# Squares over three weight blocks, a unit in three visits, two accumulators moved, a bias put behind

## The chip, the cores and the metric

The kernel runs on one core of a Trainium2 chip. The metric is the device time of one execution in microseconds: 1636.31 us, the median of three runs (1636.26 to 1636.46). The engines are named as the profile names them: PE (TensorE) with its weight loads PEld, DVE (VectorE), ACT (ScalarE), POOL (GpSimd) and SP (SyncE, which issues the loads).

## The reference

One decoder layer on 288 tokens (256 of a prompt, 8 x 4 of samples), all in float32, width 2048. Cut to what the change touches:

```python
mod = (silu(c) @ w_ada + b_ada).reshape(n, 6, 1, 2048)   # sh_m, sc_m, gt_m, sh_f, sc_f, gt_f
h = rms(x, g_mix) * (1 + sc_m) + sh_m                     # rms: x * rsqrt(mean(x*x) + eps) * gain
proj = h @ w_in                                           # 2048 x 9216, split into seven parts
```

After it come a convolution mixer, a spatial gating mixer, their merge, an output projection and a feed-forward network; the change leaves all of those as they are.

## The kernel before

Activations lie transposed: 128 features on the partitions, 288 tokens along the row, 16 feature tiles (`k`) for the width of 2048. A matmul takes 128x128 weights and a row of 288 tokens (298 where ten columns more are carried along). Full float32 precision is made from two halves: every weight `w` and every activation `a` is split into a rounded `hi` and a remainder `lo`, and a *triple* of matmuls adds `wh*ah`, `wh*al` and `wl*ah` into one accumulator in PSUM (`triple`, L248). For the weights, ACT makes `hi` (a cast) and DVE makes `lo` (a subtraction), four 128x128 parts at a time (`feed`, L267). A finished accumulator is copied out by ACT or DVE (`sinkA`; `ON_VECTOR` lists the tiles that DVE takes). Seven buffers of 1 MB (`raw`) hold loaded weights.

The head of the program, some 70 us, has its order written out by hand for PE, ACT, DVE and SP:

- The condition `c` goes through silu into `cs` (L151 to L153), and *units* of the modulation (`ada`, L407) multiply it with their weights. The first, `a0`, is the first real work of PE, after 24 fill matmuls (`warm`); it and the second, `a1`, give the first two feature tiles their scale and shift (`scaled_tile`). The third unit, `aC` (eight blocks), gives features 2 to 4 theirs; a run of its blocks between weight blocks is a *visit*.
- The square sum that the normalisation needs is not there yet when PE starts. So the first 48 output tiles of `w_in` are multiplied for features 0 and 1 with input that is scaled but not normalised (*rootless*), and the normalisation is applied to the sums later. The weight blocks in order: `w0` (feature 0, 16 output tiles), `wK` (feature 1 for the last six of those), then `wA` in blocks of eight output tiles with two triples each: four rootless blocks (output tiles 16 to 47), then three whose input is normalised (`h1`).
- `squares1` says after which tile of which block ACT squares a group of feature tiles of `x`, and DVE adds the squares up. Its two buffers are two of the seven weight buffers. `root` then queues the sums over features (`sums1`, matmuls with ones, L202), the diagonal matrix of the roots (`diagonal`) and its broadcast over the partitions (`norm1`, L235), each after a number of triples; `norm1` starts the normalised input of features 0 and 1.
- `SquareSum` and what follows the head are not changed.

PSUM has four accumulators called main, three called misc and one for the units. In `w0`, tiles 0 to 3 use all four main ones, and tiles 4 and 5 wait for two of them to be read out.

A load is issued seven steps ahead of its use, in the order of the steps, and SP issues in that order only: a load that waits for its buffer holds all behind it. A weight block's parts are split when no more than `lead` triples of given parts are left (12 unless it says otherwise); the cast then stands in ACT's queue ahead of the evictions that come after it.

Of the kernel before, what the change touches and what calls it, by code (L numbers as in the profile page):

```python
# [11 lines left out]
ALU = mybir.AluOpType  # L12
# [9 lines left out]
NC = 9  # L22
# [28 lines left out]
SINGLE = 10  # L51
FIRST = 16
ROOTLESS = 48
LATER = 48
ON_VECTOR = (2, 5, 7, 9, 10, 12, 14, 16, 18, 20, 21, 22, 24, 28)
XCUT = (0, 1, 2, 6, 10, 14, 16)

STREAMS = {
# [37 lines left out]
def _body(tc, nc, d, pc, pw, pslot, ptmp, pps):  # L96
# [15 lines left out]
    def psmain():  # L112
        return pps.tile([P, 512], F32, tag="main", name=nm("pm"), bufs=4)

    def psmisc():
        return pps.tile([P, 512], F32, tag="misc", name=nm("px"), bufs=3)

    V, A, G, PE, SY = nc.vector, nc.scalar, nc.gpsimd, nc.tensor, nc.sync
# [7 lines left out]
    bada = cp1[:, C_BADA : C_BADA + 96]  # L126
# [23 lines left out]
    ctt = const("ctt", [P, 16, NC])  # L150
    A.activation(ctt, ct, AF.Tanh, scale=0.5)  # L151
    V.scalar_tensor_tensor(ctt, ctt, 1.0, ct, ALU.add, ALU.mult)
    V.tensor_scalar(cs[:, :, :NC], ctt, 0.5, None, ALU.mult)  # L153
    mod = const("mod", [P, 96, NC])
    gm1 = const("gm1", [P, 16, NC])
    gm2 = const("gm2", [P, 16, NC])
# [1 line left out]
    end = const("end", [P, 2, TU - TP])  # L158
    G.memset(end, 0.0)
    bada1 = const("bada1", [P, 2])  # L160
    V.tensor_scalar(bada1, bada[:, 16:18], 1.0, None, ALU.add)


    class SquareSum:
# [3 lines left out]
        def add(self, a, cuts=((0, T),)):  # L168
            q = tmp() if self.last is not None else ptmp.tile([P, T], F32, tag="acc", name=nm("acc"), bufs=1)
            for o, e in cuts:  # L170
                A.activation(q[:, o:e], a[:, o:e], AF.Square)  # L171
            if self.last is not None:
                if self.acc is None:
                    self.acc = self.last
                else:
                    V.tensor_tensor(self.acc, self.acc, self.last, ALU.add)  # L176
            self.last = q
# [115 lines left out]
    def later(f, gap=0):  # L293
        if not pending:
            since[0] = 0
        pending.append((f, gap))
# [6 lines left out]
    def behind(a, b):  # L303
        tc.add_manual_dep(
            a.ins,
            b.ins.name,
            mybir.DependencyInfo(mybir.DependencyClass.NoSync, mybir.DependencyReason.DATA),
            reason="program order",
        )
# [228 lines left out]
    class OneTile(Blk):  # L538
        held = {}

        def run(self):
            a, turn, hooks = self.rhs(self.k0), [], self.hooks
            (ah, al) = a
            for j in range(self.nm):
                if (self.name, j) == ("w0", 0):
                    pss = [psmain() for _ in range(4)]
                    for i, ps in enumerate(pss):
                        PE.matmul(ps[:, :TU], self.parts[i][0], ah, start=True, stop=False)
                    for i, ps in enumerate(pss):
                        PE.matmul(ps[:, :TU], self.parts[i][1], ah, start=False, stop=False)  # L550
                if self.name == "wK":
                    ps = OneTile.held.pop(j)
                    triple(ps[:, :TU], self.parts[j], a, False, True, True)
                elif j < 4:
                    ps = pss[j]
                    PE.matmul(ps[:, :TU], self.parts[j][0], al, start=False, stop=True)
                    counted()
                else:
                    ps = psmisc() if SINGLE <= j < FIRST - 4 else psmain()
                    triple(ps[:, :TU], self.parts[j], a, True, j < SINGLE, True)  # L560
                if self.name == "wK" or j < SINGLE:
                    self.sink(j, ps)
                    evicted(self, j)
                else:
                    OneTile.held[j - SINGLE] = ps
                drain()
                for f in hooks.get(j, ()):
                    f()
# [51 lines left out]
    def squares1():  # L620
        qa, qb = (pw.tile([P, 2048], F32, tag="raw", name=nm("q"), bufs=RAW) for _ in range(2))
        for q in (qa, qb):
            G.memset(q[:, 7 * T : 7 * T + 1], 0.0)

        def part_of(q, o, n):
            return q[:, o * T : (o + n) * T].rearrange("p (k t) -> p k t", t=T)

        q1, q0, q2, q4 = part_of(qa, 0, 4), part_of(qa, 4, 2), part_of(qb, 0, 4), part_of(qb, 4, 2)

        def square(q, a, b):  # L630
            return lambda: A.activation(q, x[:, a:b, :], AF.Square)

        def add(o, q):
            return lambda: V.tensor_tensor(o, o, q, ALU.add)

        S["sq"] = q1[:, 0]
        return {
            ("wK", 0, 4): square(q0, 0, 2),
            ("wA", 0, 0): square(q1, 2, 6),
            ("wA", 0, 1): add(q1[:, 0:2], q0),  # L640
            ("wA", 0, 2): square(q2, 6, 10),
            ("wA", 0, 3): add(q1, q2),
            ("wA", 0, 5): square(q2, 10, 14),
            ("wA", 0, 6): square(q4, 14, 16),
            ("wA", 0, 7): add(q1, q2),
            ("wA", 1, 0): add(q1[:, 0:2], q1[:, 2:4]),
            ("wA", 1, 2): add(q1[:, 0:2], q4),
            ("wA", 1, 4): add(q1[:, 0], q1[:, 1]),
        }

    def sums1():
# [13 lines left out]
    def pre_h1(k0, k1):  # L665
        def scaled(k):
            def f():
                made[k] = normed(k, S["rb1"])

            return f  # L670

        return Do(lambda: jobs.extend(scaled(k) for k in range(k0, k1)), None)
# [59 lines left out]

    def first_tile():
        low = []
        ev = a0[1].copied()
        w0.split(1, low)
        warm(2)
        scaled_tile(0, ev, lambda: low[0]())
        w0.split(1)
        S["given"], S["used"] = 8, 0  # L740
        S["feed"] = [w0, wK] + wA + wB + wX + wS + wC
# [15 lines left out]
    def mk_h1(k0, k1):  # L757
        def f():
            gm_of(k0, k1)
            if S.get("paced") is not None:  # L760
                return make_h1(k0, k1)
            modulate(range(k0, k1), lambda k: normed(k, S["rb1"]), gm1, 0, h1)

        return Do(f)
# [3 lines left out]
    def sinkA(m, ps):  # L768
        t = slot(shape=(P, TU) if m < ROOTLESS else (P, T))
        part[m] = t[:, :T]  # L770
        w = T
        if m < ROOTLESS:
            raws[m], w = t, TU
        if m not in ON_VECTOR if m < 32 else m % 2 or m % 8 == 4:
            A.copy(t[:, :w], ps[:, :w])  # L775
        else:
            V.tensor_copy(t[:, :w], ps[:, :w])
# [269 lines left out]
    for b in wA[:many]:  # L1047
        b.width = TU
    w0.cut = 512
    w0.lead, wK.lead, wA[0].lead, wA[1].lead = 6, 3, 4, 6  # L1050
    wA[0].cut = wA[1].cut = wA[2].cut = 1024

    steps = [Do(lambda: warm(24)), a0[0], Do(lambda: warm(8)), a0[1]]
    steps += [Do(first_tile), Do(lambda: warm(6))]

    def root():
        later(sums1, 1)
        later(lambda: diagonal(S["r1"]), 6)
        later(norm1, 4)

    plan = {4: [Do(root, None)], 5: aC[:4], 6: [pre_h1(2, 5)], 7: aC[4:] + [mk_h1(2, 5)]}
    steps += at([w0, wK] + wA, plan)
    steps += at(wB, {2: aD[:4], 3: [pre_h1(5, 8)], 4: aD[4:] + [mk_h1(5, 8)]})
    free = Do(lambda: None, None)
# [214 lines left out]
```

## Time and profile before

| | |
|---|---|
| median of three runs | 1636.31 us |
| the profiled execution's own time | 1637.67 us |
| its span, first to last instruction | 1635.9 us |
| PE busy | 1621.4 us (99%) |
| PE weight loads busy | 1547.1 us (95%) |
| DVE busy | 1016.8 us (62%) |
| ACT busy | 739.7 us (45%) |
| granted TensorE clock, mean | 0.998 |

Times in the views are microseconds from the span's start. In a timeline a row gives start, length, engine, line, operation, what is written and read (buffer numbers left out), the count of merged instructions, and in brackets the idle time of the engine ahead of it with the one that ended it. A row of grouped instructions gives busy time and mean nanoseconds of one, then the idle time ahead. A row of waits gives the total, the count and the longest. Matmuls overlap: one lasts 0.30 us in the records, while the next starts 0.13 to 0.14 us after it. A row of DMA issues gives size and time from issue to landing.

### The profile page before, as it was taken

The numbers are of one execution on the slowest core, as the hardware profiler recorded it, in microseconds if no ns is written. First come the engines' busy times: TensorE is split into PE (matmuls) and PEld (weight loads), VectorE is DVE, ScalarE is ACT, GpSimd is POOL, SyncE is SP. The second block draws the span as 40 slices with busy tenths as digits, with TensorE's granted clock in tenths as the row PEclk, the third lists the DMA queues.
The fourth block names the chain that finished last, engine by engine and source line by source line (L and its number), as shares of the span: only waits on it lengthen the run. The fifth ranks groups of instructions, "written<-read, shape, count | busy, mean of one in ns | idle before, by whom it ended". The sixth has DMA issues, their size and how long they took to land.

```text
span 1635.9 us, 31039 instructions
## 1 busy us (share of the span) xinstructions
PE 1621.4 (99%) x12353; PEld 1547.1 (95%) x12353; DVE 1016.8 (62%) x2191; ACT 739.7 (45%) x1364; POOL 20.8 (1%) x66
## 2 busy tenths in 40 slices
PE   9999999999999999999999999999999999999997
PEld 7899899988998999999998999999999999999997
DVE  5677688877755567667844555555555555555565
ACT  5543344643444434456743444444444444444453
POOL 0000000000000000011000000000000000000000
PEclk9999999999999999999999999999999999999999
DMA  8877775767786767744576556543464434644341
GB/s 342 316 309 277 293 265 204 265 255 281 291 316 258 277 243 287 270 165 158 209 304 252 199 169 208 177 155 124 160 219 168 163 125 160 224 156 172 111 156 58
DMA packets 59425, 357.57 MB, mean 219 GB/s; under 512 B 6640, under 2 KB 9872, under 8 KB 28560
## 3 DMA queue, kind: packets, MB, share of 16 engines
q1 hardware_dynamic: 58992, 355.45, 59.1%
q8 instruction: 96, 1.57, 0.4%
q14 instruction: 49, 0.40, 0.1%
q10 hardware_dynamic: 288, 0.15, 0.0%
HBM read 352.48 MB, written 3.09 MB: 217 GB/s over the span
## 4 chain that ended last, share of the span: by engine, by line
PE 96%; DMA 1%; DVE 1%; ACT 1%; issue 0%; DVEq 0%; ACTq 0%
PE pm L250 30%; PE pm L253 30%; PE pm L255 30%; PE ada L418 5%; DMA raw<-in_wA 1%; DMA cp<-in_cpack 0%; DVE x L1020 0%; PE pm L618 0%; ACT hi L500 0%; PE px L250 0%; PE px L253 0%; PE px L858 0%; DVE lo L506 0%; PE px L202 0%; PE px L899 0%
## 5 line engine op out<-in xcount | busy, mean ns | idle before, releaser
L250 PE MATMUL pm<-s,hi 128*128 128x288 f32 (+1 forms) x3752 | 1110.1, 296 | 1.3 <-ACT s L775 1.3
L253 PE MATMUL pm<-s,hi 128*128 128x288 f32 (+1 forms) x3752 | 1106.4, 295 | 0.2 <-DVE s L345 0.2
L255 PE MATMUL pm<-s,lo 128*128 128x288 f32 (+1 forms) x3738 | 1102.3, 295 | 0.6 <-DVE lo L269 0.5
L500 ACT CAST hi<-raw 128x512 fp32r<-128x512 f32 (+1 forms) x963 | 588.5, 612 | 815.8 <-PE pm L253 791.6
L506 DVE TENSOR_TENSOR lo<-raw,hi 128x512 fp32r<-128x512 f32 (+1 forms) x849 | 578.4, 681 | 448.2 <-ACT hi L500 430.8
L250 PEld LDWEIGHTS pm<-s,hi 128*128 128x128 f32 x3752 | 706.0, 188 | 21.2 <-issue 15.7
L253 PEld LDWEIGHTS pm<-s,hi 128*128 128x128 f32 x3752 | 705.5, 188 | 0.5 <-DVE s L345 0.4
L255 PEld LDWEIGHTS pm<-s,lo 128*128 128x128 f32 x3738 | 703.4, 188 | 1.3 <-DVE lo L269 1.3
L269 DVE TENSOR_TENSOR lo<-raw,hi 128x512 fp32r<-128x512 f32 (+1 forms) x113 | 75.8, 673 | 33.1 <-ACT hi L500 32.2
L418 PE MATMUL ada<-raw,cs 128*32 128x512 f32 (+2 forms) x832 | 88.4, 563 | 0.5 <-DVE cs L153 0.5
L418 PEld LDWEIGHTS ada<-raw,cs 128*32 128x32 f32 x832 | 24.1, 109 | 46.7 <-issue 43.6
L806 DVE TENSOR_TENSOR s<-pm,s 128x288 f32<-128x288 f32 x72 | 32.8, 456 | 14.5 <-PE pm L255 14.4
L362 DVE SCALAR_TENSOR_TENSOR x<-pm,mod,x 128x256 f32<-128x256 f32 x80 | 38.0, 475 | 2.7 <-PE pm L255 2.7
L319 ACT CAST s<-t 128x288 fp32r<-128x288 f32 (+1 forms) x76 | 32.6, 433 | 12.5 <-DVE t L838 5.8
L321 DVE TENSOR_TENSOR s<-t,s 128x288 fp32r<-128x288 f32 (+1 forms) x76 | 34.6, 458 | 5.9 <-ACT s L319 5.9
L985 DVE SCALAR_TENSOR_TENSOR t<-t,pm 128x288 f32<-128x288 f32 x42 | 19.1, 454 | 16.0 <-PE pm L255 16.0
L798 DVE TENSOR_TENSOR s<-pm,s 128x288 f32<-128x288 f32 x48 | 21.8, 454 | 10.7 <-PE pm L255 9.5
L368 DVE TENSOR_TENSOR t<-pm,mod 128x32 f32<-128x32 f32 x80 | 15.3, 191 | 18.1 <-PE pm L255 18.0
L783 DVE SCALAR_TENSOR_TENSOR s<-pm,s 128x256 f32<-128x256 f32 x48 | 23.0, 480 | 4.1 <-PE pm L255 4.1
L171 ACT ACTIVATE t<-x 128x288 f32<-128x288 f32 (+2 forms) x31 | 13.5, 437 | 20.5 <-DVE x L371 17.3
L789 DVE TENSOR_TENSOR s<-s,rb 128x288 f32<-128x288 f32 x48 | 21.5, 447 | 0.0
L176 DVE TENSOR_TENSOR acc<-acc,t 128x288 f32<-128x288 f32 x34 | 15.4, 454 | 8.2 <-ACT t L171 8.2
(150 smaller groups left out, 482.1 us busy)
## 6 DMA issues: line engine op xcount, KB each, us to landing
raw<-in_fi SPq DMA_DIRECT2D x84, 1024.0 KB, 4.9
raw<-in_a SPq DMA_DIRECT2D x64, 1024.0 KB, 9.2
raw<-in_f SPq DMA_DIRECT2D x64, 704.0 KB, 4.1
raw<-in_wD SPq DMA_DIRECT2D x36, 1024.0 KB, 4.9
raw<-in_aE SPq DMA_DIRECT2D x16, 1024.0 KB, 10.0
raw<-in_wo SPq DMA_DIRECT2D x16, 1024.0 KB, 5.0
raw<-in_wC SPq DMA_DIRECT2D x19, 768.0 KB, 4.4
raw<-in_pa SPq DMA_DIRECT2D x8, 1024.0 KB, 5.0
```

Source lines behind the costliest of these rows:

```text
L250: PE.matmul(out, wh, ah, start=first, stop=False)
L253: end_ = PE.matmul(out, wh, al, start=False, stop=turn and last)
L255: end_ = PE.matmul(out, wl, ah, start=False, stop=last)
L269: lows.pop(0)[1]()
L319: A.copy(hi, a)
L321: V.tensor_tensor(lo, a, hi.bitcast(F32), ALU.subtract)
L362: V.scalar_tensor_tensor(x[:, m, :TP], ps[:, :TP], mod[:, gt0 + m, 0:1], x[:, m, :TP], ALU.mult, ALU.add)
L418: PE.matmul(acc[32 * j : 32 * j + 32, :w], cs[:, kt, :], self.raw[:, o : o + w], start=(kt < ks), stop=(kt >= 16 - ks), tile_position=(0, ...
L500: A.copy(hi, self.raw[:, s * 128 : e * 128])
L506: sub()
L783: V.scalar_tensor_tensor(t[:, :TP], ps[:, :TP], t[:, T : T + 1], t[:, :TP], ALU.add, ALU.add)
L806: V.tensor_tensor(a, ps[:, :T], a, ALU.add)
```

## The change

Four edits, all in the head. The operation that adds one to the bias of the first scales (`bada1`) is issued later, and told to stand behind the one that writes `cs`. Tiles 4 and 5 of `w0` take misc accumulators. The squares and their additions are put at other tiles, the last two additions in the third `wA` block, with the sums ten triples into that block; the leads of the first two `wA` blocks and the list of the tiles that DVE copies out change with them (20 of the 48 rootless tiles were DVE's, now 21). The eight blocks of the third unit come in visits of two, three and three, after the third, fourth and fifth `wA` block, in place of four and four after the third and fifth.

```diff
@@ -52,7 +52,7 @@
-ON_VECTOR = (2, 5, 7, 9, 10, 12, 14, 16, 18, 20, 21, 22, 24, 28)
+ON_VECTOR = (2, 5, 7, 9, 10, 12, 14, 18, 19, 22, 23, 26, 27, 30, 32, 35, 37, 41, 43, 45, 47)
@@ -150,7 +150,7 @@
-    V.tensor_scalar(cs[:, :, :NC], ctt, 0.5, None, ALU.mult)
+    cs_made = V.tensor_scalar(cs[:, :, :NC], ctt, 0.5, None, ALU.mult)
...
-    V.tensor_scalar(bada1, bada[:, 16:18], 1.0, None, ALU.add)
@@ -556,7 +555,7 @@
-                    ps = psmisc() if SINGLE <= j < FIRST - 4 else psmain()
+                    ps = psmisc() if SINGLE <= j < FIRST - 4 or j < 6 else psmain()
@@ -636,16 +635,16 @@
             ("wK", 0, 4): square(q0, 0, 2),
-            ("wA", 0, 0): square(q1, 2, 6),
-            ("wA", 0, 1): add(q1[:, 0:2], q0),
-            ("wA", 0, 2): square(q2, 6, 10),
-            ("wA", 0, 3): add(q1, q2),
-            ("wA", 0, 5): square(q2, 10, 14),
-            ("wA", 0, 6): square(q4, 14, 16),
+            ("wA", 0, 1): square(q1, 2, 6),
+            ("wA", 0, 3): add(q1[:, 0:2], q0),
+            ("wA", 0, 5): square(q2, 6, 10),
             ("wA", 0, 7): add(q1, q2),
-            ("wA", 1, 0): add(q1[:, 0:2], q1[:, 2:4]),
-            ("wA", 1, 2): add(q1[:, 0:2], q4),
-            ("wA", 1, 4): add(q1[:, 0], q1[:, 1]),
+            ("wA", 1, 1): square(q2, 10, 14),
+            ("wA", 1, 3): add(q1, q2),
+            ("wA", 1, 4): square(q4, 14, 16),
+            ("wA", 1, 6): add(q1[:, 0:2], q1[:, 2:4]),
+            ("wA", 2, 0): add(q1[:, 0:2], q4),
+            ("wA", 2, 3): add(q1[:, 0], q1[:, 1]),
@@ -732,6 +731,7 @@
     def first_tile():
         low = []
+        behind(V.tensor_scalar(bada1, bada[:, 16:18], 1.0, None, ALU.add), cs_made)
@@ -771,7 +771,7 @@
-        if m not in ON_VECTOR if m < 32 else m % 2 or m % 8 == 4:
+        if m not in ON_VECTOR if m < ROOTLESS else m % 2 or m % 8 == 4:
@@ -1047,18 +1047,18 @@
-    w0.lead, wK.lead, wA[0].lead, wA[1].lead = 6, 3, 4, 6
+    w0.lead, wK.lead, wA[0].lead, wA[1].lead = 6, 3, 6, 8
...
     def root():
-        later(sums1, 1)
+        later(sums1, 10)
...
-    plan = {4: [Do(root, None)], 5: aC[:4], 6: [pre_h1(2, 5)], 7: aC[4:] + [mk_h1(2, 5)]}
+    plan = {4: [Do(root, None)], 5: aC[:2], 6: aC[2:5] + [pre_h1(2, 5)], 7: aC[5:] + [mk_h1(2, 5)]}
```

**SP's queue from the third unit's first block on.** `in_aC` is the third unit, `in_wA` the weight blocks, the first of them here the fourth rootless one. Before:

```order
L400 DMA raw_164<-in_aC 128x1536
L400 DMA raw_183<-in_aC 128x1536
L400 DMA raw_230<-in_aC 128x1536
L400 DMA raw_363<-in_aC 128x1536
L484 DMA raw_404<-in_wA 128x2048
L484 DMA raw_502<-in_wA 128x2048
L400 DMA raw_602<-in_aC 128x1536
```

Now:

```order
L399 DMA raw_163<-in_aC 128x1536
L399 DMA raw_182<-in_aC 128x1536
L483 DMA raw_230<-in_wA 128x2048
L399 DMA raw_366<-in_aC 128x1536
L399 DMA raw_405<-in_aC 128x1536
L399 DMA raw_502<-in_aC 128x1536
L483 DMA raw_600<-in_wA 128x2048
```

The fourth rootless block's load moves ahead of two of the unit's blocks, and the next weight block's load moves behind one more of them. The buffers move with it: the fourth rootless block takes that of the first (`raw_121`), and the one after it takes that of the first squares (`q_123`).

**DVE's queue around the sums.** `q` are the squares, `lo` the remainders of weights, `s<-pm` the copies out of accumulators, `e<-px` the first operation on the finished sums. Before (`raw_131` and `raw_136` are the second and third rootless block):

```order
L634 TENSOR_TENSOR q_124<-q_124,q_125 128x1152
L777 COPY s_514<-pm_504 128x298
L634 TENSOR_TENSOR q_124<-q_124 128x576
L269 TENSOR_TENSOR lo_513<-raw_131,hi_511 128x512
L634 TENSOR_TENSOR q_124<-q_124,q_125 128x576
L269 TENSOR_TENSOR lo_536<-raw_131,hi_534 128x512
L269 TENSOR_TENSOR lo_539<-raw_136,hi_537 128x512
L269 TENSOR_TENSOR lo_554<-raw_136,hi_552 128x512
L777 COPY s_565<-pm_557 128x298
L634 TENSOR_TENSOR q_124<-q_124 128x288
L269 TENSOR_TENSOR lo_577<-raw_136,hi_575 128x512
L215 TENSOR_SCALAR e_613<-px_608 128x3
```

Now (`raw_135` is the third rootless block, `raw_230` the fourth):

```order
L633 TENSOR_TENSOR q_123<-q_123,q_124 128x1152
L268 TENSOR_TENSOR lo_550<-raw_135,hi_548 128x512
L268 TENSOR_TENSOR lo_574<-raw_135,hi_572 128x512
L777 COPY s_585<-pm_577 128x298
L633 TENSOR_TENSOR q_123<-q_123 128x576
L268 TENSOR_TENSOR lo_597<-raw_135,hi_595 128x512
L777 COPY s_610<-pm_602 128x298
L633 TENSOR_TENSOR q_123<-q_123,q_124 128x576
L268 TENSOR_TENSOR lo_622<-raw_230,hi_620 128x512
L777 COPY s_645<-pm_635 128x298
L633 TENSOR_TENSOR q_123<-q_123 128x288
L268 TENSOR_TENSOR lo_644<-raw_230,hi_642 128x512
```

The last three additions stood among the remainders of the second block and the first of the third; now they stand behind all remainders of the third block, and the last one behind the first remainder of the fourth. Lines of the changed kernel between L161 and L734 are lower by one.

## The prediction

> **What bounds the kernel now.** The page came first: who ends last.
>
> ```profile
> PE 96%; DMA 1%; DVE 1%; ACT 1%; issue 0%; DVEq 0%; ACTq 0%
> ```
>
> The chain of waits is TensorE's own work, so a change of order can only gain what TensorE waits, and it moves no instruction after about 68 us. The view of TensorE's waits from 75 us to the end has as its longest:
>
> ```profile
> PE pm L253 <- DVE s L345: 0.2, 1, 0.2
> ```
>
> Everything to be had is therefore earlier. The timeline of weight loads shows each of those waits, with the idle time in brackets:
>
> ```profile
> 15.93 0.19 PEld L250 LDWEIGHTS pm<-s,hi 128*128 128x128 f32 x1 [0.33 <-ACT s L775]
> 16.76 0.19 PEld L250 LDWEIGHTS pm<-s,hi 128*128 128x128 f32 x1 [0.39 <-ACT s L775]
> 25.03 0.19 PEld L252 LDWEIGHTS px<-s,lo 128*128 128x128 f32 x1 [0.52 <-DVE lo L269]
> 31.19 0.19 PEld L255 LDWEIGHTS pm<-s,lo 128*128 128x128 f32 x1 [0.21 <-DVE lo L269]
> 33.66 0.19 PEld L255 LDWEIGHTS pm<-s,lo 128*128 128x128 f32 x1 [0.78 <-DVE lo L269]
> 38.90 0.19 PEld L255 LDWEIGHTS pm<-s,lo 128*128 128x128 f32 x1 [0.28 <-DVE lo L269]
> 47.73 0.19 PEld L250 LDWEIGHTS pm<-s,hi 128*128 128x128 f32 x1 [1.05 <-ACT s L775]
> 49.01 0.30 PEld L235 LDWEIGHTS px<-t,ones 128*128 128x128 f32 x2 [0.84 <-DVE t L229]
> 65.58 0.19 PEld L250 LDWEIGHTS pm<-s,hi 128*128 128x128 f32 x1 [0.53 <-ACT s L775]
> ...
> 64.98 0.29 PE L255 MATMUL pm<-s,lo 128*128 128x288 f32 x1
> 65.58 0.40 PE L250 MATMUL pm<-s,hi 128*128 128x288 f32 x1 [0.30 <-ACT s L775]
> ```
>
> The last two rows scale the brackets. The matmuls start 0.60 apart where 0.13 is the step, so the wait costs 0.46; the weight load's bracket says 0.53. I take 0.08 off each bracket. The matmul after a wait takes 0.40 instead of 0.30, so a restart costs another 0.10. The wait at 25.03 stands behind the second scaled tile, whose rows do not move; I leave it as it is.
>
> **The change, part by part.**
>
> *Bias put behind.* At the start:
>
> ```profile
> 1.23 5.88 PE L618 MATMUL pm<-wb 128*128 128x288 bf16 x24 [1.23 <-POOL wb L612]
> 5.47 0.32 ACT L151 ACTIVATE ctt<-ct 128x144 f32<-128x144 f32 x1 [2.54 <-DMA ct<-in_c]
> 6.91 0.17 DVE L161 TENSOR_SCALAR bada<-cp 128x2 f32<-128x2 f32 x1 [5.35 <-DMA cp<-in_cpack]
> 7.64 1.07 PE L418 MATMUL ada<-raw,cs 128*32 128x256 f32 x16 [0.53 <-DVE cs L153]
> 8.64 1.16 PE L618 MATMUL pm<-wb 128*128 128x288 bf16 x8
> 9.72 0.64 PE L418 MATMUL ada<-raw,cs 128*32 128x256 f32 x8
> 10.30 0.91 PE L618 MATMUL pm<-wb 128*128 128x288 bf16 x6
> ...
> raw<-in_a SPq DMA_DIRECT2D x1, 512.0 KB, 5.5
> ```
>
> VectorE stands at L161 until the second constant pack lands (6.91), and `cs` queues behind it; TensorE starts the first unit at 7.64. Moved behind, the two operations that make `cs` start when ScalarE is done (5.79); they took from 7.08 to 7.64, so `cs` is there at about 6.4. The 24 fill matmuls have a step of 5.88/24 = 0.245, the last one starting near 6.73, so the unit can start at about 7.03: **0.60 gained**. Its second half of weights, issued at 1.2, lands 5.5 later (last row), in time. What comes after hangs on engines that were waiting for TensorE, and moves with it.
>
> *Two small accumulators.* Tiles 4 and 5 of the first block no longer wait for the evictions of tiles 0 and 1: 0.25 + 0.10 at 15.93 and 0.31 + 0.10 at 16.76, **0.76**. Tile 6 now starts at the old 16.5, when the eviction that released the row at 15.93 is long done.
>
> *Squares spread.* The waits at 31.19, 33.66 and 38.90 are halves of weights (`lo`) that VectorE makes late, behind wide additions and a queue of squares on ScalarE: 0.12 + 0.10, 0.70 + 0.10, 0.20 + 0.10. The durations:
>
> ```profile
> 39.44 1.89 DVE L269 TENSOR_TENSOR lo<-raw,hi 128x512 fp32r<-128x512 f32 x3
> L777 DVE COPY s<-pm 128x298 f32<-128x298 f32 x15 | 6.8, 461 | 2.4 <-PE pm L255 2.2 <-PE pm L253 0.2
> L634 DVE TENSOR_TENSOR q<-q,q 128x1152 f32<-128x1152 f32 x2 | 2.7, 1353 | 0.1
> L634 DVE TENSOR_TENSOR q<-q 128x576 f32<-128x576 f32 x2 | 1.5, 752 | 0.3 <-ACT q L631 0.3
> L631 ACT ACTIVATE q<-x 128x1152 f32<-128x1152 f32 x3 | 3.5, 1174 | 0.1
> 47.28 0.40 ACT L775 COPY s<-pm 128x298 f32<-128x298 f32 x1
> ...
> 42.01 0.30 PE L250 MATMUL pm<-s,hi 128*128 128x298 f32 x1
> 42.42 0.72 PE L202 MATMUL px<-ones,q 128*128 128x1 f32 x6
> 43.00 0.38 PE L250 MATMUL pm<-s,hi 128*128 128x298 f32 x1
> ```
>
> Three matmuls take 0.41 (42.01 to 42.42), a tile of six 0.825. With the gains so far every `lo` of the first two rootless blocks is written 0.4 us or more before its matmul, so all three waits go: **1.32**. Together 2.68: the third rootless block, at 42.01 before, starts at 39.33; the first, 16 tiles earlier, at 26.13.
>
> The price is what is late next. The last addition stands three tiles into the third block, and the sums wait for it after tile 5 (39.33 + 5 x 0.825 = 43.46). VectorE's queue to there: the second tile of the first block ends at 27.78; its eviction, the square of 1152 columns and a cast follow on ScalarE, 0.20 + 0.30 + 1.07 + 0.62 (each starts 0.1 before the one ahead ends), so the cast is there at 29.97. From then VectorE has 24 operations without a break, each starting 0.08 before the one ahead ends (three in 1.89): ten `lo` at 0.605, eight evictions at 0.38, two additions at 1.27, three at 0.67 and the last, a quarter as wide as the 1.27, at 0.45: 14.1. The sum is there at 44.1, 0.65 after TensorE; with a restart **0.75 lost**. Bounds: nothing, if a few operations start earlier than I have them; 1.3, if one more 1152-wide addition's worth of delay comes in.
>
> *Root later, unit in 2, 3, 3.* The wait at 49.01 (0.76, the diagonal late behind VectorE) goes: in the new order ten more triples and a visit lie between sums and broadcast. The one at 47.73 is a load:
>
> ```profile
> 46.76 0.62 ACT L500 CAST hi<-raw 128x512 fp32r<-128x512 f32 x1 [3.75 <-DMA raw<-in_wA]
> 40.15 0.41 SPq L484 DMA_DIRECT2D raw<-in_wA  x1
> raw<-in_wA SPq DMA_DIRECT2D x1, 1024.0 KB, 6.5
> raw<-in_wA SPq DMA_DIRECT2D x1, 1024.0 KB, 10.3
> ```
>
> ScalarE stood at a cast for the fourth rootless block's weights, issued at 40.15 behind four loads of the unit, and the evictions queued behind the cast. Now that load stands ahead of the unit's third and takes the first rootless block's buffer, free when its last `lo` is made (30.7). With 6.5 or 10.3 to landing (the third and fourth rows: the issues at 40.15 and 54.22) it is there at 37 to 41; ScalarE reaches the cast at 39.9 and an eviction behind it is wanted only after four more tiles. The wait goes: **0.97 + 0.10**. The load after next, for the first block with normalised input, now needs the buffer of the squares, free after the sums (44.9, behind the unit's loads); 6.5 later, 51.4, it is in time: the fourth block starts at 48.8, and TensorE wants the third copy behind that cast after the broadcast and six tiles, at 54.4; cast and copies take 1.4. Covered; each microsecond later than 53 costs one.
>
> The third visit is extra:
>
> ```profile
> 51.77 2.79 PE L418 MATMUL ada<-raw,cs 128*32 128x384 f32 x32
> 54.48 0.41 PE L250 MATMUL pm<-s,hi 128*128 128x298 f32 x1
> ```
>
> A visit's fixed part: 0.10 going in, 0.10 restart, and the way out, from the first unit's rows above: 16 records 1.00, 8 records 0.58, so 0.16 that does not scale. **0.35 lost.** Four blocks take 2.71 from first record to the next matmul, a visit of three about 2.07.
>
> The wait at 65.58 stays, for another reason:
>
> ```profile
> 64.61 0.62 ACT L500 CAST hi<-raw 128x512 fp32r<-128x512 f32 x1 [2.46 <-DMA raw<-in_wA]
> 52.68 0.33 SPq L400 DMA_DIRECT2D raw<-in_aC  x1
> raw<-in_fi SPq DMA_DIRECT2D x84, 1024.0 KB, 4.9
> ```
>
> That load now waits for a buffer of the second visit, free 0.91 after the visit's start (52.68 against 51.77), lands 4.9 later with the queue empty, and TensorE resumes 1.0 after (64.61 to 65.58): visit + 6.85. It wants the eviction at visit + 2.07 + 0.10 + five tiles of 0.794 = 6.13. So 0.72 instead of 0.46, **0.26 lost**; bounds 0 and 1.0. The Trainium skill (DMA: Bandwidth & Descriptors, section on the anatomy of one DMA) has about 2.0 us plus bytes over 436 GB/s for a transfer issued by GpSimd, an estimate of 4.4 here; by it this loss would be a gain of 0.24 and the sum 3.7. The 84 loads of this trace measure 4.9, and I keep that.
>
> **Sum.** Gains 0.60 + 0.76 + 1.32 + 0.76 + 1.07 = 4.51; losses 0.75 + 0.35 + 0.26 = 1.36: 3.15 off. The profiled execution took 1637.67 (span 1635.89, 1.8 around it), which becomes 1634.5; it is 1.36 above the median of the runs, and the median 1636.31 becomes **1633.1**. A measurement of this kernel can tell about 0.2%, 3.3 us, from no change; my forecast lies right at that edge, just inside.
>
> **The rivals.**
>
> *The two new losses do not come* (sums in time, load in time): 4.51 - 0.35 = 4.2 with the last wait as before, 4.7 without it: 1632.1 to 1631.6; half of it, 3.9, counts here too. For: the lateness of 0.65 is the end of 24 operations, and 3% off them moves it by 0.4. Against: the widths and the order are known.
>
> *VectorE's backlog reaches the evictions.* It also empties accumulators in that stretch, each only about 0.6 us before TensorE wants it (tile 3 of the third block: read by 40.5, wanted at 41.0). A backlog 1 us longer makes a second and third wait: gain 1.0 to 2.4, 1633.9 to 1635.3. For: VectorE has no idle time from 30 to 44; against: that is counted.
>
> *The clock comes late.* The fill matmuls step by 0.245 and the next eight by about 0.13, so the change of rate fell between 6.7 and 7.64, the very time into which the first unit moves. If it falls after 7.03, the unit runs part of its 0.9 us at half rate and 0.3 to 0.5 of the 0.60 is lost: gain 2.7, 1633.6. The Trainium skill (TensorE: Matmul & The Clock Gate, Part 1) says that the full rate follows a busy window that runs freely and that the point shifts by 500 ns from run to run; that speaks against counting on the 0.60. For the rule is that the rows show the switch; against the rival, that the last fill matmul is followed by a unit that was at full rate when it began.
>
> *Slower.* The load of the normalised block waits for the sums; if the sums or the queue hold it past 53, ScalarE's cast holds the evictions and every microsecond is TensorE's. From 56.2 on all is given back; at 57, 1637. That needs 12 us from issue, against 10.3 as the worst row.
>
> **How the numbers follow.** Forecast 0.51 (its own range 1632.5 to 1633.7), losses absent 0.20, backlog 0.20, clock 0.05, slower 0.04. The edge is at 1633.04: of the forecast some 45% lies below it, with the second case 0.43 faster; slower by over 0.2% 0.03; the rest 0.54 within. The range takes the forecast, most of the case below and most of the backlog: 1631.9 to 1634.9.
>
> **What would show it.** The first unit at about 7.0; no weight-load wait near 16, 31, 33 and 38; at the sums a wait of some 0.65 for the last addition, near 43.5; no wait of a cast for the fourth rootless block; none before the broadcast; a wait of about 0.7 in the middle of the first normalised block, near 62, for a load issued 0.9 after the second visit began. A wait in the third rootless block other than at the sums, or a cast waiting past 53, would prove the sum wrong.

## The result, and the profile after

| | before | after |
|---|---|---|
| median, 15 runs each, us | 1636.27 (1636.06 to 1637.14) | 1633.07 (1632.53 to 1633.60) |
| ratio of the times, 95% interval | | 0.998 (0.9972 to 0.9988) |
| profiled execution: time, span, us | 1637.67, 1635.9 | 1633.44, 1631.6 |

The change makes the kernel 3.20 us faster, 0.196%: just inside the 0.2% that the prediction took as the edge (1633.04 on its reckoning). Forecast were 1633.1 us and 3.15 (1636.31 - 3.15 is 1633.16).

A place behind the head shows what the head gave. The timeline of matmuls has, between 88 and 99 us, the same four blocks of a later unit behind the same work in every kernel. Before:

```profile
94.02 2.79 PE L418 MATMUL ada<-raw,cs 128*32 128x384 f32 x32
```

After:

```profile
90.79 2.79 PE L417 MATMUL ada<-raw,cs 128*32 128x384 f32 x32
```

3.23 us earlier; this row is called the *landmark* below. The two spans differ by 4.3, so 1.0 lies in later code, whose order is the same in both. The profiled execution of before was 1.40 above its median and that of after 0.37: the difference, 1.03, is about that 1.0. The medians and the landmark agree; the spans of the two single executions don't measure the change. That this 1.0 belongs to the two executions and not to the change is not shown: in the kernels tried below, the span has gained on before between 0.0 us (two accumulators alone) and 2.0 us (all edits) more than the landmark, and no view of TensorE's waits behind 99 us has one over 0.3 us.

The timeline of weight loads of after has, from 23 us up to 48, these rows with a wait behind another engine in brackets (the next, at 48.49 with 0.62, is the first load behind a visit, where before has the same 0.62 at 54.48):

```profile
23.32 0.19 PEld L251 LDWEIGHTS px<-s,lo 128*128 128x128 f32 x1 [0.52 <-DVE lo L268]
43.71 0.74 PEld L201 LDWEIGHTS px<-ones,q 128*128 128x128 f32 x6 [0.90 <-DVE q L633]
```

The waits of before near 16, 31, 33, 38, 47 and 49 are gone, the one at the second tile is where it was, and the sums have a new one. Two more follow, in the timelines of weight loads and of matmuls:

```profile
54.20 0.19 PEld L249 LDWEIGHTS pm<-s,hi 128*128 128x128 f32 x1 [0.24 <-ACT s L775]
...
62.98 0.40 PE L249 MATMUL pm<-s,hi 128*128 128x288 f32 x1 [0.60 <-ACT s L775]
```

Both are evictions behind a cast that waited for a load. ScalarE's timeline has the casts, and the list of loads the time from issue to landing of the two loads, issued at 44.57 and 57.00:

```profile
52.92 0.62 ACT L499 CAST hi<-raw 128x512 fp32r<-128x512 f32 x1 [2.89 <-DMA raw<-in_wA]
62.01 0.62 ACT L499 CAST hi<-raw 128x512 fp32r<-128x512 f32 x1 [3.95 <-DMA raw<-in_wA]
...
raw<-in_wA SPq DMA_DIRECT2D x1, 1024.0 KB, 8.2
raw<-in_wA SPq DMA_DIRECT2D x1, 1024.0 KB, 4.9
```

For the sums, the chain of waits from 42.31 us on (start, length, engine, what is written, line) is VectorE without a gap to the last addition, and TensorE starts at its end:

```profile
42.31 0.60 DVE lo L268
42.91 0.38 DVE s L777
43.29 0.38 DVE q L633
43.67 0.04 issue
43.71 0.83 PE px L201 x6
```

### The profile page after: what moved, and what is told of

It reads as the page before. It is cut to its first block, busy times and chain, and to the rows that moved or that the text cites. A ratio compares the mean times of both kernels' runs of the same rounds, so it can differ in the third digit from the quotient of the medians.

```text
span 1631.6 us, 31028 instructions
## 1 busy us (share of the span) xinstructions
PE 1618.9 (99%) x12353; PEld 1545.5 (95%) x12353; DVE 1016.2 (62%) x2192; ACT 739.3 (45%) x1363; POOL 20.8 (1%) x66
## 3 DMA queue, kind: packets, MB, share of 16 engines
HBM read 352.48 MB, written 3.09 MB: 218 GB/s over the span
## 4 chain that ended last, share of the span: by engine, by line
PE 98%; DVE 1%; DMA 0%; issue 0%; ACT 0%; DVEq 0%; POOL 0%; ACTq 0%; POOLq 0%
PE pm L249 30%; PE pm L252 30%; PE pm L254 30%; PE ada L417 5%; PE pm L617 1%; DMA raw<-in_wA 0%; DVE x L1020 0%; PE px L201 0%; PE px L249 0%; PE px L252 0%; DVE q L633 0%; PE px L858 0%; DVE lo L505 0%; PE px L899 0%; PE px L254 0%
```

## The experiments

The theory is that of the prediction: the time is TensorE's work plus its waits in the head, so that each part of the change is worth the waits that it removes less those that it makes. The rival is that a removed wait is mostly taken up by the next one, so that the parts alone bring little. The kernels ran in four groups, each with the kernel before beside it (1636.29, 1636.36, 1636.46 and 1636.54 us; 1636.27 beside the change itself); differences of medians are against that one. Landmarks are of one execution each, and in the kernels with the bias put behind they also move with the start of the first unit, 6.36 to 6.97 us.

| kernel | median, us | less than before | ratio, 95% interval | landmark |
|---|---|---|---|---|
| the change | 1633.07 | 3.20 | 0.998 (0.9972 to 0.9988) | 90.79 |
| bias alone | 1635.55 | 0.74 | 0.9996 (0.9987 to 1.0004) | 92.32 |
| two accumulators alone | 1635.65 | 0.64 | 0.9996 (0.9987 to 1.0005) | 92.61 |
| squares alone | 1642.04 | 5.75 more | 1.0035 (1.0022 to 1.0048) | 98.60 |
| visits alone | 1634.61 | 1.68 | 0.999 (0.9981 to 0.9999) | 92.71 |
| change + later casts | 1632.95 | 3.41 | 0.9978 (0.9969 to 0.9987) | 90.17 |
| change + evictions to ACT | 1632.80 | 3.56 | 0.9975 (0.9965 to 0.9984) | 89.86 |
| both of these | 1632.10 | 4.26 | 0.9971 (0.996 to 0.9983) | 89.19 |
| change + fewer fill matmuls | 1632.90 | 3.46 | 0.9978 (0.9969 to 0.9987) | 90.27 |
| change without squares | 1632.86 | 3.60 | 0.9976 (0.9967 to 0.9984) | 91.02 |
| squares and visits | 1634.85 | 1.61 | 0.9989 (0.9981 to 0.9998) | 92.12 |
| all edits | 1630.18 | 6.28 | 0.996 (0.9947 to 0.9974) | 88.71 |
| all edits but squares | 1631.73 | 4.81 | 0.997 (0.9959 to 0.9981) | 89.84 |

The intervals reach some 1.3 to 2.3 us to each side, wider than most single steps, and those of the bias alone and of the accumulators alone include 1; the waits in the traces carry the argument there, the medians the total.

### The parts alone

**The bias**, on the kernel before:

```diff
-    V.tensor_scalar(cs[:, :, :NC], ctt, 0.5, None, ALU.mult)
+    cs_made = V.tensor_scalar(cs[:, :, :NC], ctt, 0.5, None, ALU.mult)
...
-    V.tensor_scalar(bada1, bada[:, 16:18], 1.0, None, ALU.add)
...
+        behind(V.tensor_scalar(bada1, bada[:, 16:18], 1.0, None, ALU.add), cs_made)
         ev = a0[1].copied()
```

> The kernel before with the bias operation put behind, alone. My theory: the first unit starts when the 24 fill matmuls are through, at 6.7 to 7.05 in place of 7.64, and all that follows moves with it: 0.6 to 0.95 us off, about 1635.5; the runs spread wider than those of before (some 1 us), since the start now hangs on when the fill matmuls come to full rate. Rival: what follows waits for loads anyway, so no gain (1636.3).

0.74 off by the medians, as expected; the runs spread over 2.0 us (1635.14 to 1637.13). The unit starts at 6.56, behind `cs`, in place of 7.64, and the later waits of the head stay (weight loads of this kernel):

```profile
6.56 0.59 PEld L417 LDWEIGHTS ada<-raw,cs 128*32 128x32 f32 x16 [0.52 <-DVE cs L153]
...
32.56 0.19 PEld L254 LDWEIGHTS pm<-s,lo 128*128 128x128 f32 x1 [0.81 <-DVE lo L268]
```

So the earlier start isn't taken up by the next waits: they move with it, as the prediction has it.

**The accumulators:**

```diff
-                    ps = psmisc() if SINGLE <= j < FIRST - 4 else psmain()
+                    ps = psmisc() if SINGLE <= j < FIRST - 4 or j < 6 else psmain()
```

> The kernel before with tiles 4 and 5 of the first block in the small accumulators, alone. My theory: the weight-load waits at 15.93 and 16.76 go with their restarts, 0.76 us, 1635.5, and nothing takes their place. Rival: the next eviction or weight half is late in their place and 0.2 us or less is left (1636.1).

0.64 off by the medians; in the trace the waits at 15.93 and 16.76 are gone and none stands in their place.

In both, the landmark says more than the median: 1.70 and 1.41 ahead of that of before. The last of the head's waits, near 65 in before, is absent from both, with nothing of the change near it. Its load was issued about 1 us earlier there and landed 2 us earlier; ScalarE's cast behind it, 64.61 before, is here in the kernel with the bias alone:

```profile
62.44 0.62 ACT L499 CAST hi<-raw 128x512 fp32r<-128x512 f32 x1 [1.41 <-DMA raw<-in_wA]
```

The profiled execution of before, 1637.67 us, was longer than each of the 15 runs (1636.06 to 1637.14) and seems to have had a slow load at that place; whether its median execution has this wait was not measured.

**The squares**, with their list of tiles, leads and the sums ten triples into the block:

```diff
...
-            ("wA", 0, 0): square(q1, 2, 6),
...
+            ("wA", 2, 0): add(q1[:, 0:2], q4),
+            ("wA", 2, 3): add(q1[:, 0], q1[:, 1]),
...
-        later(sums1, 1)
+        later(sums1, 10)
```

> The kernel before with the squares spread, the new evictions, leads and the sums ten triples in, but visits of four and four. My theory: the parts do not add up. The three waits for weight halves go (1.3 us), but the fourth rootless block's load now takes the third one's buffer and is issued near 43 in place of 40.2, so the wait for it grows from 1.0 to some 2.5 us, beside a wait for the sums: 0 to 0.5 us off, 1635.8 to 1636.3. Rival (parts add up): 1.32 + 0.76 - 0.8 = 1.3 us off, 1635.0.

5.75 slower, outside both expectations. The three waits for `lo` are gone, but the sums come far too late. Timelines of this kernel, VectorE's and ScalarE's, then weight loads:

```profile
43.20 0.74 DVE L634 TENSOR_TENSOR q<-q,q 128x576 f32<-128x576 f32 x1
48.60 0.69 DVE L269 TENSOR_TENSOR lo<-raw,hi 128x512 fp32r<-128x512 f32 x1 [4.65 <-ACT hi L500]
49.21 0.46 DVE L777 COPY s<-pm 128x298 f32<-128x298 f32 x1
49.59 0.45 DVE L634 TENSOR_TENSOR q<-q 128x288 f32<-128x288 f32 x1
...
47.95 0.62 ACT L500 CAST hi<-raw 128x512 fp32r<-128x512 f32 x1 [6.49 <-DMA raw<-in_wA]
...
50.09 1.36 PEld L202 LDWEIGHTS px<-ones,q 128*128 128x128 f32 x6 [5.64 <-DVE q L634]
```

The last addition stands behind the fourth rootless block's first `lo`; that needs the cast, and the cast the load, which without the new visits is issued at 42.94, behind the unit's loads. The expectation had the issue right and did not follow what stands behind the cast on VectorE. And the idle time has a second price, in the busy time and granted clock by stretches (busy us and instructions of each engine, then the clock):

```profile
44.50:50.00 5.50, 0.19 (x2) 0.00 (x0) 1.40 (x4) 2.05 (x5) 0.00 (x0) 0.90 0.88 369
50.00:53.00 3.00, 2.91 (x12) 2.91 (x13) 0.80 (x3) 0.01 (x1) 0.86 (x1) 0.50 0.28 43
53.00:56.00 3.00, 3.00 (x13) 2.83 (x12) 1.58 (x4) 1.06 (x3) 0.00 (x0) 0.54 0.55 225
56.00:59.00 3.00, 3.00 (x35) 1.22 (x35) 0.69 (x1) 0.89 (x2) 0.00 (x0) 1.00 0.36 102
```

After 5.4 us of idle TensorE the clock is at half. (Microsecond by microsecond, the same view has it at 0.97 from 48 to 49 and at 0.50 from 49 to 50, some 4 us after the last matmul began at 44.40.) The matmuls then step by 0.25 (first and last of 18 in the timeline of matmuls, and what follows them):

```profile
51.39 0.59 PE L250 MATMUL pm<-s,hi 128*128 128x298 f32 x1
...
55.76 0.31 PE L255 MATMUL pm<-s,lo 128*128 128x298 f32 x1
56.00 2.79 PE L418 MATMUL ada<-raw,cs 128*32 128x384 f32 x32
```

18 matmuls take 4.61 instead of 18 x 0.1375 = 2.48, 2.1 lost. The sums take 1.30 from their start to the next matmul (50.09 to 51.39); in after they take 0.69:

```profile
43.71 0.83 PE L201 MATMUL px<-ones,q 128*128 128x1 f32 x6 [0.65 <-DVE q L633]
44.40 0.38 PE L249 MATMUL pm<-s,hi 128*128 128x298 f32 x1
```

That is 0.6 more, so 2.7 in all, on top of the wait. The Trainium skill (TensorE: Matmul & The Clock Gate, Part 1) says that the clock falls to half after an idle window of about 3.4 us. This trace agrees: 5.4 us idle brought 0.50, while the waits of up to 1 us in the kernels before and after left it at 1.00.

**The visits:**

```diff
-    plan = {4: [Do(root, None)], 5: aC[:4], 6: [pre_h1(2, 5)], 7: aC[4:] + [mk_h1(2, 5)]}
+    plan = {4: [Do(root, None)], 5: aC[:2], 6: aC[2:5] + [pre_h1(2, 5)], 7: aC[5:] + [mk_h1(2, 5)]}
```

> The kernel before with the unit's visits of two, three and three, alone. My theory: the fourth rootless block's load is issued near 33.6 and the wait at 47.73 (1.07 us) goes, and with it the wait at 49.01 (0.76), whose operations on the vector engine stood behind the same load; a third visit costs 0.35 and the wait near 65 grows by 0.26: 1.2 us off, 1635.1. Rival: the wait at 49.01 is of the vector engine's own and stays: 0.46 off, 1635.8.

1.68 off, 1.31 by the landmark; 1.2 was expected. Both waits, 47.73 and 49.01, are gone: the matmuls of the broadcast follow the one ahead of them by 0.13.

```profile
46.97 0.30 PE L255 MATMUL pm<-s,lo 128*128 128x298 f32 x1
47.10 0.65 PE L235 MATMUL px<-t,ones 128*128 128x288 f32 x2
...
64.94 0.40 PE L250 MATMUL pm<-s,hi 128*128 128x288 f32 x1 [0.69 <-ACT s L775]
```

The last row is the last wait of the head, which stays. So the wait of the broadcast, 0.76, which the prediction gave to the visits and the later root together, goes with the visits alone; the kernels with the bias alone and the accumulators alone keep it. That fits one cause for both waits: the late load held the cast, and VectorE's work for the diagonal came after it. VectorE's timeline of before has that order, the remainder behind the late cast and then the diagonal (L229):

```profile
47.41 0.69 DVE L269 TENSOR_TENSOR lo<-raw,hi 128x512 fp32r<-128x512 f32 x1 [3.09 <-ACT hi L500]
...
48.73 0.23 DVE L229 TENSOR_SCALAR t<-cp,r 128x32 f32<-128x32 f32 x1
```

### The two waits that are left, and the fill

**Later casts.** A smaller `lead` puts the casts of the first two normalised blocks behind more evictions in ScalarE's queue:

```diff
+    wA[4].lead = wA[5].lead = 6
     wA[0].cut = wA[1].cut = wA[2].cut = 1024
```

> The changed kernel, with the weights of the first two normalised blocks split when six triples of given parts are left in place of twelve. My theory: the waits at 54.20 (0.26 with its restart) and 62.98 (0.88) come from the cast's place in the scalar engine's queue, ahead of evictions, not from the loads being late for their own matmuls; a later cast finds its load landed and both waits go: 1.1 us off, 1632.0. Rival: the loads are late for their own use, the wait moves to the start of the block and nothing is gained (1633.1).

The waits at 54.20 and 62.98 are gone. The one at 62.98 stays in each kernel with the change's visits that leaves the casts where they were (62.48 with fewer fill matmuls), so the place of the cast made it. The one at 54.20 is absent from several of those too, so it shows less: it may be of the one execution. And casts moved on into the tiles after the last visit, where two small new waits stand (matmuls of this kernel, start 0.31 and 0.37 after the one ahead, where 0.13 is the step):

```profile
73.36 0.30 PE L254 MATMUL pm<-s,lo 128*128 128x288 f32 x1
73.67 0.40 PE L249 MATMUL pm<-s,hi 128*128 128x288 f32 x1
...
74.45 0.30 PE L254 MATMUL pm<-s,lo 128*128 128x288 f32 x1
74.82 0.40 PE L249 MATMUL pm<-s,hi 128*128 128x288 f32 x1
```

0.62 of the landmark remains, and 0.2 of the median, where 1.1 was expected. The expectation missed the new waits: here the rival, that the next wait takes up what was gained, holds for part of the gain.

**Evictions to ScalarE.** Three tiles of the third rootless block's time leave VectorE's list:

```diff
-ON_VECTOR = (2, 5, 7, 9, 10, 12, 14, 18, 19, 22, 23, 26, 27, 30, 32, 35, 37, 41, 43, 45, 47)
+ON_VECTOR = (2, 5, 7, 9, 10, 12, 14, 18, 19, 22, 23, 26, 27, 37, 41, 43, 45, 47)
```

> The changed kernel, with the evictions of output tiles 30, 32 and 35 given to the scalar engine. My theory: the vector engine's queue ahead of the last addition is 1.1 us shorter, so the wait for the sums (0.81 and its restart) goes: 0.9 off, 1632.2. Rival: the load of the first normalised block, which stands behind the queue of loads and lands at 52.8, keeps its time, so the wait in the fourth rootless block grows from 0.26 to about 1.1 and nothing is gained (1633.1).

The last addition now ends 0.6 before TensorE wants it, and the sums follow in step (VectorE's timeline and that of the matmuls):

```profile
42.34 0.45 DVE L633 TENSOR_TENSOR q<-q 128x288 f32<-128x288 f32 x1
...
43.26 0.30 PE L254 MATMUL pm<-s,lo 128*128 128x298 f32 x1
43.39 0.73 PE L201 MATMUL px<-ones,q 128*128 128x1 f32 x6
```

That shows the reason of the wait: VectorE's 24 operations in one row, and nothing that they wait for. The landmark is 0.93 earlier, but not by this wait alone: the wait at 54.20 (0.26) is missing too and the last one is 0.15 shorter (0.69 against 0.84 in the brackets of the weight loads), while the unit of this execution started 0.27 later than that of after. The median is only 0.36 lower by the differences, where 0.9 was expected.

**Both** of these edits in one kernel:

> The two edits of the later casts and the evictions together. If each wait is local: 1.1 + 0.9 = 2.0 us off, 1631.1. If the load takes back what the sums give: with the later cast there is nothing for it to take back, so the two together still give 2.0 while the evictions alone give little. If the loads are late for their own use: 0.9 at most.

Landmark 1.60 earlier, median 4.26 below before, 1.06 more than the change; 2.0 was expected. That the landmarks add up (0.62 + 0.93) is chance in part: each kernel alone lacks the wait at 54.20, which can go only once, and the unit starts at 6.55 here, 6.60 with the casts and 6.97 with the evictions. The medians of the two alone give 0.21 + 0.36. The waits do add up: neither the sums nor 62.98 has one here, and the two small new ones are there, at 72.69 and 73.83.

**Fewer fill matmuls:**

```diff
-    steps = [Do(lambda: warm(24)), a0[0], Do(lambda: warm(8)), a0[1]]
+    steps = [Do(lambda: warm(20)), a0[0], Do(lambda: warm(8)), a0[1]]
```

> The changed kernel with 20 fill matmuls ahead of the first unit in place of 24. My theory: the unit starts when the fill matmuls are through, whose time hangs on when full rate comes; with four fewer (0.96 us at the slow step) it starts when its second half of weights has landed, about 6.7, in every run: 0 to 0.3 us off in the median and a narrower spread of the runs (some 0.5 us in place of 1.1). Rival: with less work the full rate comes later, the unit and what follows run slow: 0.3 us or more longer.

Landmark 0.52 earlier, median 0.26 lower by the differences, and the runs spread over 0.66 us in place of 1.07. Only 0.13 of the landmark is the start of the unit (6.57 against 6.70); this execution, too, lacks the wait at 54.20. The fill is over before `cs` is there (matmuls of this kernel):

```profile
1.23 4.19 PE L617 MATMUL pm<-wb 128*128 128x288 bf16 x20 [1.23 <-POOL wb L611]
6.57 1.07 PE L417 MATMUL ada<-raw,cs 128*32 128x256 f32 x16 [1.15 <-DVE cs L153]
```

### What the squares are worth

The squares bring a wait for the sums and take away three for `lo`. Two kernels, the change without the squares (bias, accumulators and visits), and the squares with the visits alone. The first, on the kernel before:

```diff
...
+        behind(V.tensor_scalar(bada1, bada[:, 16:18], 1.0, None, ALU.add), cs_made)
...
+                    ps = psmisc() if SINGLE <= j < FIRST - 4 or j < 6 else psmain()
...
+    plan = {4: [Do(root, None)], 5: aC[:2], 6: aC[2:5] + [pre_h1(2, 5)], 7: aC[5:] + [mk_h1(2, 5)]}
```

> The changed kernel with the squares, evictions, leads and the sums put back as before: the bias, the two accumulators and the visits alone. By the parts measured alone (0.74, 0.64 and 1.68 us) 3.06 off: 1633.2, as the whole change. That is my theory: with the visits changed the waits for weight halves (1.3 us and more) are traded for the wait at the sums, the one in the fourth rootless block and little else, so the spread squares bring 0.3 us or less. Rival, my prediction's own sum: without them the waits for weight halves stay and the sums' wait is saved, 1.32 - 0.75 = 0.6 us longer than the change: 1633.7.

The second, on the kernel before:

```diff
...
+            ("wA", 2, 3): add(q1[:, 0], q1[:, 1]),
...
+        later(sums1, 10)
...
+    plan = {4: [Do(root, None)], 5: aC[:2], 6: aC[2:5] + [pre_h1(2, 5)], 7: aC[5:] + [mk_h1(2, 5)]}
```

> The kernel before with the squares (and their evictions, leads, sums) and the visits, without the bias and the accumulators. Alone the squares cost 5.7 us, by a load that came too late for a cast in front of the last additions; with the visits that load is early. My theory: 1.8 us off, 1634.5, and no wait over 1 us at the sums. Rival: the 5.7 is a cost of the squares' own places, and the two together are about 4 us longer than before (1640).

Without squares 3.60 off, not less than the 3.20 of the whole; squares and visits 1.61, not more than the 1.68 of the visits alone. Beside the visits the squares no longer cost 5.75: the wait at the sums is 0.67 in its bracket, in place of 5.64. By the landmarks the squares are worth 0.23 (91.02 to 90.79) and 0.59 (92.71 to 92.12). The waits for `lo` are there without them, as before:

```profile
29.44 0.19 PEld L254 LDWEIGHTS pm<-s,lo 128*128 128x128 f32 x1 [0.21 <-DVE lo L268]
31.92 0.19 PEld L254 LDWEIGHTS pm<-s,lo 128*128 128x128 f32 x1 [0.82 <-DVE lo L268]
37.16 0.19 PEld L254 LDWEIGHTS pm<-s,lo 128*128 128x128 f32 x1 [0.34 <-DVE lo L268]
```

So in the change the squares trade these 1.4 us (restarts included) for a wait of 0.9 and what comes with it; the time that is left can't be told from nothing.

**All edits:** the change with the evictions on ScalarE, 20 fill matmuls, and leads of 8 (12 in the change, 6 in the kernel with later casts), so that the casts stand between the two places that had waits.

```diff
-ON_VECTOR = (2, 5, 7, 9, 10, 12, 14, 18, 19, 22, 23, 26, 27, 30, 32, 35, 37, 41, 43, 45, 47)
+ON_VECTOR = (2, 5, 7, 9, 10, 12, 14, 18, 19, 22, 23, 26, 27, 37, 41, 43, 45, 47)
...
+    wA[4].lead = wA[5].lead = 8
...
-    steps = [Do(lambda: warm(24)), a0[0], Do(lambda: warm(8)), a0[1]]
+    steps = [Do(lambda: warm(20)), a0[0], Do(lambda: warm(8)), a0[1]]
```

> The changed kernel with the three evictions on the scalar engine, 20 fill matmuls, and the weights of the first two normalised blocks split at eight triples left (six in the run before, where two new waits of 0.3 each came near 74 from casts that had moved there). My theory: the earlier cast takes those two waits away as well and the start is at 6.6: 1631.5. Rival: at eight the cast again stands ahead of evictions while its load is on the way and 0.5 or more of a wait comes back: 1632.1 or more.

1630.18 us, 6.28 below before: faster than before and after, and 1.3 below the 1631.5 that was expected. The view of TensorE's waits to 91 us has only the start, the first two tiles and `cs` left:

```profile
PE pm L617 <- POOL wb L611: 1.2, 1, 1.2
PE pm L547 <- ACT s L724: 0.3, 1, 0.3
PE px L251 <- DVE lo L268: 0.3, 1, 0.3
PE ada L417 <- DVE cs L153: 0.3, 1, 0.3
```

Its landmark is 5.31 earlier than that of before, 1 us less than the medians say, and its span is 7.3 us shorter. Where the rest lies, in later code whose order is the same, was not found.

**All edits but the squares** has the squares and the tiles on VectorE as before, and bias, accumulators and visits as in the change. Beside those, on the kernel before:

```diff
+    wA[4].lead = wA[5].lead = 8
...
-    steps = [Do(lambda: warm(24)), a0[0], Do(lambda: warm(8)), a0[1]]
+    steps = [Do(lambda: warm(20)), a0[0], Do(lambda: warm(8)), a0[1]]
```

> The kernel before with the bias behind, the two small accumulators, the visits of 2, 3 and 3, leads of 8 for the two last rootless blocks' successors and 20 fill matmuls: the kernel with all edits but with the squares (and the tiles that DVE copies out) as they were before. Theory (the squares edit is worth its three waits for `lo`, about 1.4 us, once the wait at the sums that it brings is taken away, as it is in the kernel with all edits): those three waits are there again near 29, 31 and 37, and the time is about 1.4 above that kernel's 1630.2, so 1631.6. Rival (the squares edit is worth nothing beside the visits even then, since TensorE's later waits take up what was gained): within 0.4 of 1630.2.

1631.73, 4.81 below before: 1.47 less gained than with the squares, 1.13 by the landmark. The three waits are there (0.20, 0.81 and 0.33 in brackets), none at 54 or 62. Once the wait at the sums is taken away (by the three evictions), the squares are worth about what the prediction's term of 1.32 says; with it, about nothing.

## Why the prediction was right, and where it wasn't

The total, 3.15 forecast and 3.20 measured, agrees better than its terms do: the bias gave 0.34 more, the waits that stayed or came took 0.47 more, and that these nearly cancel is luck.

| term | forecast, us | after, by its trace, us |
|---|---|---|
| bias behind | +0.60 | +0.94 |
| accumulators | +0.76 | +0.76 |
| waits for `lo` | +1.32 | +1.32 |
| broadcast | +0.76 | +0.76, but by the visits |
| load of the fourth rootless block | +1.07 | +1.07 |
| wait at the sums | -0.75 | -0.90 |
| extra visit | -0.35 | -0.33 |
| last wait | -0.26 | -0.32 |
| wait at 54.20 | none | -0.26 |
| sum | 3.15 | 3.04 (landmark 3.23) |

For the four waits that are gone the trace of after shows only that they are gone; their sizes are those of before's rows. From the first weight loads of `w0` to the next unit block the accumulators' term can be read in the timelines of weight loads: 3.86 us in before (13.92 to 17.78), 3.09 in after (12.98 to 16.07), 0.77 less.

- *Bias.* The unit starts at 6.70 instead of 7.03 (matmuls of after; the unit is the second row).

```profile
1.23 5.54 PE L617 MATMUL pm<-wb 128*128 128x288 bf16 x24 [1.23 <-POOL wb L611]
6.70 1.07 PE L417 MATMUL ada<-raw,cs 128*32 128x256 f32 x16
```

  The step that failed is that all 24 fill matmuls keep their step of 0.245; they took 5.54 us here against 5.88, so the last of them came faster. In the kernel with the squares alone, where 24 took 4.72, the view by microseconds counts 6 of them in each from 2 to 4 and 8 in each from 4 to 6. That the clock came to full rate there is inferred from this pace; the column of the granted clock reads 1.00 from 1 us on. In the kernel with the evictions on ScalarE they took 5.81, and the unit started at 6.97; so the size of this term differs from one execution to the next. The rival of the late clock did not come: the unit's 16 records take 1.07 here as in before.
- *Sums.* The mechanism and the place were right, VectorE busy from 29.64 to 43.66, 14.0 us for the 14.1 of the sum. TensorE was there at 42.90 (0.81 and a restart of 0.09 against 0.65 and 0.10). The runs without the wait show that it is VectorE's backlog alone; the rival in which the backlog reaches the evictions too did not come, nor the one in which this loss is absent.
- *The normalised block's load.* Reckoned to land at 51.4, it landed at about 52.8: 8.2 us after its issue, where 6.5 was taken. That is 0.2 before the 53 from which the prediction let it cost, but the point was a little too late: the copy behind the cast came 0.16 late, with a restart 0.26. This load is the one on which the slower rival rests; from 56.2 on it would have taken all the gain.
- *Last wait.* 0.77 and 0.11 for 0.72 and 0.10; the load took the 4.9 us that the row of 84 loads gave. The estimate of 4.4 from the Trainium skill (DMA: Bandwidth & Descriptors, section on the anatomy of one DMA), whose formula is for transfers issued by GpSimd and by which this term would be a gain, is 0.5 too short for this one, issued by SyncE.
- *Visit.* From the first record to the next matmul the two old visits took 2.71 + 2.72, the three new ones 1.42 + 2.07 + 2.07; with 0.20 for one more start and restart that is 0.33 more.
- *Root later.* Here the attribution was wrong. The prediction puts "ten more triples and a visit" between sums and broadcast. In the timelines of matmuls ten triples lie there in after (from 44.40 on) and ten in before (from 43.00 on); only the visit is new. And with the visits alone, where the first visit (49.72) comes behind the broadcast (47.10), the wait is gone all the same, since the load that held ScalarE's cast is early. The later root and the spread squares are then worth 1.32 - 0.90 - what the later waits take, not 0.57 and 0.76, and the whole change is no faster by the medians than the same without them.
- *The offset.* The prediction took the 1.36 by which the profiled execution of before was above its median as the same for both kernels; the profile of after is 0.37 above its own. Two parts of the 1.36 can be named, but not proved: the last wait of before (0.46 and a restart of 0.10), which the executions of the bias alone and of the accumulators alone lack, and later code, which took 0.8 us longer in before than with the bias alone (spans 2.5 apart, landmarks 1.70). If the median execution lacks that last wait, the change removed less in the head than the sum says, and the forecast came out right with errors that cancel. This was not settled.

## What to carry to other kernels

Where one engine is busy 99% of the span, sum its waits one by one from the timeline, with their restarts, and measure the result at a landmark behind the changed code and not only by the spans of two executions; but read the landmark beside the rows ahead of it, since one execution's start or a late load moves it too. Before two waits are given two causes, ask whether the second engine was itself held by the first cause: a part tried alone tells it, and here one part of the change turned out to bring nothing until its own new wait was removed. When an operation is put later in an in-order queue, read everything that stands ahead of it there and what that waits for: the squares alone cost 5.75 us because the last addition came to stand behind a remainder of weights, which needs a cast, which needs a load that was late.

## What the runs showed of the hardware

Idle time costs more than its length where it is long: 5.4 us without TensorE work brought a granted clock of 0.50 and 0.54 in the two stretches of 3 us that followed, 2.7 us on top of the wait. Waits of up to 1 us did not: in before the clock reads 1.00 in each microsecond from 46 to 50, around the waits at 47.73 and 49.01.

The pace of the fill changes at a time that differs between executions: 24 fill matmuls took 5.88 us in before, 5.54 in after, 5.81 with the evictions on ScalarE, and in the kernel with the squares alone

```profile
1.24 4.72 PE L618 MATMUL pm<-wb 128*128 128x288 bf16 x24 [1.24 <-POOL wb L612]
```

A weight load of 1 MB takes 8.2 or 9.5 us where other loads are under way (those issued at 44.57 and 30.36 in after; the row is that of the second; a load of the unit issued at 42.39, ahead of the first, took 7.1) and 4.9 where none was ahead of it (issued at 57.00):

```profile
raw<-in_wA SPq DMA_DIRECT2D x1, 1024.0 KB, 9.5
```

Behind 90 us, before took 1.0 us longer than after and 2.0 us longer than all edits, with the same order of work and no wait over 0.3 us; no cause was found.
